# Last projection pair out of the stage's pool, heads split into even and odd, a later load of z, a longer wait in the gating's sums, and SiLU and splits of the projection as items of their own

## The chip, the cores and the metric

The kernel runs on one core of one Trainium2 chip. The metric is the device time of one execution in microseconds (us); several runs are taken and their median is given. A profile of one execution shows every engine: TensorE (PE, with its weight loads as PEld), VectorE (DVE), ScalarE (ACT), GpSimd (POOL), and SyncE (SP), whose queue issues the DMA transfers.

## What is computed

One inference step of one layer: a half-step SwiGLU feed-forward, a token mixer with two parallel branches, and a second half-step feed-forward, all with RMSNorm ahead and plain residual adds. There are 1024 prompt tokens of one sequence and 8 sequences with 8 sample tokens each, width 1024, feed-forward width 2816. All of it is in float32. The mixer is where the change lies:

```python
proj = hn @ w_in
u, z, xbc, dt_raw, gate_logits = ...            # 1024, 2048, 3072, 32, 2048 columns
branch_pool = pool_mix(u_ext, ...) @ pool_w_out # trailing-window means minus token, windows 2, 4, 8, 16
xbc_c, new_conv = causal_conv(xbc, ...)         # width 4, then SiLU
y, new_ssm = ssd_scan(xs, dt, A, bm, cm, ssm_h0)# 32 heads of 64 in 4 groups, chunks of 128 tokens
y = y + d_skip[:, None] * xs
yg = y * silu(z)
yg = yg * rsqrt(mean(yg * yg over a group) + EPS)
branch_ssd = (yg * ssd_norm) @ ssd_w_out
gates = sigmoid(gate_logits)
merged = gates[0] * branch_pool + gates[1] * branch_ssd
return merged @ w_o, new_pool, new_conv, new_ssm
```

The new states of the pooling, the convolution and the scan are outputs too.

## The kernel before

**Tiling.** Activations lie with features on the 128 partitions and tokens along the free axis, in two halves: h = 0 has 512 prompt tokens, h = 1 the other 512 and the 64 sample tokens, 576. A float32 product is made of three products of rounded high and low parts (`hi`, `lo` or `hl` of the activations, `wh` and `wl` of the weights). ACT makes `wh` (L443) and DVE `wl` (L444), each 128x512. The feed-forward's first matrix and the projection use one level of Winograd's form of Strassen's product: a pair of column blocks takes seven products in the order 1, 2, 6, 5, 7, 3, 4, and POOL makes the weights' sums `s` (L437) for four of them.

**Stages.** The first feed-forward runs to about 800 us, the projection to 1523 us, the mixing stage to 2125 us, and the second feed-forward to the end. The first two share one pool of buffers, in which `fx` takes one of 17 rotating tiles. The mixing stage opens a pool of its own in the same memory, so its first tiles wait for whatever was last read there. `act` takes tiles of the pool that lives through the whole program; in the mixing stage `fx` does so too.

**The projection** (`in_proj`, `proj_pair`). After `mix_dt` and some plain blocks come gate pairs, then for each of the 4 groups three convolution pairs ("c"), one pooling pair ("u") and two pairs of `z`, and at the end one gate pair for h = 1 alone. `proj_pair` asks for the seven products; `after` and `leave` evict each from PSUM as it ends (copies on ACT, additions on DVE, h = 0's sums on POOL) with a raised priority of 40 places in the program's order, as for `wh` and `wl`. When a block is whole, `done` puts an item on the list `work`: `post_conv` (for each block and half one ACT pass, three DVE passes L940 over the row `ct`, and SiLU on ACT L942 with a store), `post_u` (running sums `us` on DVE L955, on small tiles `urs` for the sample tokens L959, the difference `dd` L966, a split of it and two stores), `post_z`, `post_gate`, and `state_out` (PE transposes `pst` of the last rows, then stores).

**What sets the order.** `pe[0]` is a clock of PE's work as the program is written, counted by `mm`. Generators started as a `Chain` are stepped by `tick` when that clock passes their due time; the number that a generator yields is its wait. `worker` takes items of `work` in order, each not before RIPE us of that clock after it was posted. At the start of a pair `proj_pair` sets `hurry` and steps the worker until no more than 4 items are on the list; all that it records then stands ahead of the pair. A scheduler then lays out each engine's row from the recorded order and the priorities. Every engine, and SP's DMA queue, runs its row in order.

**The mixing stage.** `pool_branch` multiplies the differences `d` by the group weights (`pgm`), then by the output weights `pool_w_out` (`pbp`). Beside it runs the chain `scan`: for each half and group it fetches `dts`, `bc` (B and C rows) and `xs` (L1518 to L1526) and walks the chunks. `ssd_a` loads `ab`, the running sums of dt times A of the group's heads, broadcast to all partitions, from the scratch tensor `acs_d` (one tile of 4 heads at a time, two for a chunk) and makes of it `ea` (exponentials, one head per 64 partitions, L1355) and the decay matrices in `ab` itself (L1357, L1358); `ssd_b` makes `pyo` and `pyd` and the output; `ssd_st` makes the state `pst`. Gating multiplies by `z`, which `ssd_group` loads at the fourth chunk, and `rstd` sums squares over a group by the matmuls `pss` and waits for them. Then come `ssd_w_out` (`pso`), the merge of the branches (`acc`, L1595, and t1 = `t` L1608, L1609) and `w_o` (`pwo`).

Of the kernel before, what the change touches and what calls it, by code (L numbers as in the profile page):

```python
# [44 lines left out]
STEP_S = 1.0  # L45
POST, RIPE = 1.0, 3.0
GP = (1.5, 1.2)
# [14 lines left out]
def tile_hybrid_pool_ssd_macaron(  # L62
# [189 lines left out]
    acs_d = [dp.tile([4, NH, CH], F32, tag=f"acsd{h}", name=f"acsd{h}") for h in HALVES]  # L252
# [116 lines left out]
    def rstd(tiles, h, count, out, pace=1.0):  # L369

        N = NTOK[h]
        nch = 4 + h
        s = act((P, N), name="ssq")
        for i, x in enumerate(tiles):
            if i == 0:
                S.activation(s, x, AF.Square)
            else:
                q = act((P, N), name="sq")
                S.activation(q, x, AF.Square)
                V.tensor_tensor(s, s, q, op=ALU.add)  # L380
# [24 lines left out]
        yield R_WAIT  # L405
        out.append(r)
        yield 1.5
# [419 lines left out]
    def mix_dt(h, xs):  # L827
# [9 lines left out]
        def chain():  # L837
# [43 lines left out]
            dma(acs_d[h].rearrange("c h l -> (c h) l"), afm)  # L881
# [28 lines left out]
    def post(gen):  # L910
        work.append((pe[0] + RIPE, gen))
# [12 lines left out]
    def post_conv(h, ct, raw, new):  # L924
# [17 lines left out]
        S.activation(t[:, :N], t[:, :N], AF.Silu)  # L942
        dma(convd[h][ct], t[:, :N])
        yield POST / 2

    def post_u(h, k, raw, smp):
# [6 lines left out]
        while sh < w:  # L953
# [20 lines left out]
        yield POST  # L974
# [21 lines left out]
    def done(kind, i, h, raw):  # L996
# [13 lines left out]
        if kind == "c":  # L1010
            if h == 1:
                smp = new
                state_out(kind, i, raw[:, 512:579])
            post(post_conv(h, i, raw, smp))
        else:
            if h == 1:
                smp = hists.pop(("u", i))
                G.tensor_copy(smp[0][:, :, HIST:], new)
                state_out(kind, i, raw[:, 512:591])
            post(post_u(h, i, raw, smp))  # L1020
# [34 lines left out]
    def proj_pair(kind, ia, ib, xs):  # L1055
# [4 lines left out]
        while len(work) > 4:  # L1060
            poster[0].step()
# [16 lines left out]
        def after(p, i, bk):  # L1078
# [3 lines left out]
            if p == "1":  # L1082
                out[i] = {"a": fx(name="ra"), "b": fx(name="rb")}
# [216 lines left out]
    def ssd_a(h, g, c, Bf, Cf, xs4, dts, h0s):  # L1300
# [11 lines left out]
        for q in range(nq):  # L1312
            ab = act((P, hq, L), name="ab")
            if smp:
                dma(ab, acs_sd[g * HPG : (g + 1) * HPG].partition_broadcast(P))
# [35 lines left out]
        for q, ab in enumerate(abs_):  # L1351
            av = ab.rearrange("p (q h) l -> p q h l", h=2)
            ev = ea[:, q * (hq // 2) : (q + 1) * (hq // 2), :]
            for hh in range(2):
                S.activation(ev[hh * HD : (hh + 1) * HD], av[hh * HD : (hh + 1) * HD, :, hh, :], AF.Exp)  # L1355
            for i in range(hq):
                S.activation(ab[:L, i, :], ab[:L, i, :], AF.Relu, bias=acs[:L, hc + q * hq + i : hc + q * hq + i + 1], scale=-1.0)  # L1357
            S.activation(ab[:L], ab[:L], AF.Exp, scale=-1.0)  # L1358
            V.tensor_tensor(ab[:L], ab[:L], cbm[:L, :L].unsqueeze(1).broadcast_to([L, hq, L]), op=ALU.mult)  # L1359
# [10 lines left out]
    def ssd_b(h, g, c, a, hold, Cf, y4, dts, h0s):  # L1370
# [8 lines left out]
        if smp:  # L1379
# [12 lines left out]
            for i, (pr, bh) in enumerate(units):  # L1392
# [12 lines left out]
                dma(dst, h0)  # L1405
                if pr == 3:
# [19 lines left out]
        for i in range(HPG):  # L1426
            m_ = abs_[i // abs_[0].shape[1]][:L, i % abs_[0].shape[1], :]
# [31 lines left out]

    def ssd_group(h, g, Bf, Cf, xs4, dts, zs):  # L1460
# [3 lines left out]
        for c in range(4 + h):  # L1464
            ga = ssd_a(h, g, c, Bf, Cf, xs4, dts, h0s)
            next(ga)
            if c == 3:
                for j in range(4):
                    z = act((P, NTOK[h]), name="z")
                    dma(z, zd[h][g * 4 + j])  # L1470
                    zs.append(z)
# [5 lines left out]
            if prev:  # L1477
                yield from ssd_b(h, g, *prev, Cf, y4, dts, h0s)
            prev = (c, a)
        yield step  # L1480
        yield from ssd_b(h, g, *prev, ssd_st(h, g, *prev, dts), Cf, y4, dts, h0s)
# [9 lines left out]
    def gating(h, g, y4, zs, out):  # L1491
# [6 lines left out]
        yield from rstd([y4[:, j, :N] for j in range(4)], h, 512, rr, GP[0])  # L1498
# [56 lines left out]
    cs = start(scan())  # L1555

# [25 lines left out]
    def merge(h, gs, acc):  # L1582
# [18 lines left out]
        for m in range(KD):  # L1601
# [7 lines left out]
            V.tensor_tensor(t1[m], t1[m], acc[m], op=ALU.add)  # L1609
# [168 lines left out]
```

## Time and profile before

| what | before |
|---|---|
| median of 3 runs | 2938.1 us (2935.09 to 2938.73) |
| profiled execution | 2939.05 us |
| its span on the core | 2937.3 us |
| PE idle, 1000 to 1500 us (projection pairs) | 15.8 us |
| PE idle, 1523 to 2125 us (mixing stage) | 41.8 us |

A span is the time from the first to the last instruction of the profiled execution; the rest of its time lies around it. PE's idle time is the stretch less its busy time. A busy share is a mean over stages with different limits, so each stage is read by itself. In a list of waits a row has the waiting engine and line, what ended the wait, the sum of such waits in us, their number, and the longest. In a list of groups a row has line, engine, operation, tiles and shapes, count, then busy us and the mean of one in ns, then the idle time of the engine just before and what ended it. In a timeline a row has its start and duration in us, and in brackets the idle time of the engine before it.

### The profile page before, as it was taken

How to read it: one execution, taken by the hardware profiler on the slowest of the kernel's cores; microseconds unless marked ns; L12 is line 12 of the kernel's file. 1: busy time of each engine (PE TensorE's matmuls, PEld its weight loads, DVE VectorE, ACT ScalarE, POOL GpSimd, SP SyncE). 2: the span in 40 equal slices, each digit the busy share in tenths (PEclk: the TensorE clock that was granted, in tenths of full speed). 3: DMA queues.
4: the chain of work that ended last, by engine and by line, in shares of the span. 5: the costliest groups of instructions: out<-in, count | busy, mean ns of one | idle time of the engine just before them, and what ended most of it. 6: DMA issues, size and time to landing. Idle time of an engine off the chain costs nothing.

```text
span 2937.3 us, 51029 instructions
## 1 busy us (share of the span) xinstructions
PE 2828.8 (96%) x18494; PEld 2570.2 (88%) x18494; DVE 1784.7 (61%) x2843; ACT 1385.2 (47%) x3024; POOL 993.0 (34%) x1011
## 2 busy tenths in 40 slices
PE   7999999999999999999989999898999999999998
PEld 6999999789989989898977887677999999987898
DVE  6655555434484687887976877766665544453422
ACT  5444444323354555564556766566233444442422
POOL 6434444000133455454422332323234444440000
PEclk9999999999999999999999999999999999999999
DMA  4575554856445555543367777786774532236652
GB/s 134 166 224 182 160 172 132 277 188 194 112 126 163 159 179 159 183 127 124 98 221 240 235 235 232 229 271 184 237 241 153 161 98 77 81 101 212 218 156 72
DMA packets 530332, 507.97 MB, mean 173 GB/s; under 512 B 36884, under 2 KB 374664, under 8 KB 530072
## 3 DMA queue, kind: packets, MB, share of 16 engines
q1 hardware_dynamic: 530064, 504.72, 54.0%
q8 instruction: 145, 2.38, 0.3%
q14 instruction: 107, 0.88, 0.1%
q10 hardware_dynamic: 16, 0.00, 0.0%
HBM read 361.77 MB, written 143.05 MB: 172 GB/s over the span
## 4 chain that ended last, share of the span: by engine, by line
PE 44%; DVE 6%; ACT 3%; DMA 3%; issue 1%; POOL 1%; SPq 1%; POOLq 0%; ACTq 0%; DVEq 0%
PE pw L163 19%; PE po L163 9%; PE pso L163 4%; PE pwo L163 3%; PE pbp L163 3%; PE pg L163 1%; PE pu L163 1%; ACT ab L1357 1%; PE pyd L163 1%; DVE wl L444 1%; DVE ct L940 1%; PE pst L163 1%; DMA wraw<-in_ffn_w_in_dram 0%; DVE xs L1504 0%; DVE ab L1359 0%
## 5 line engine op out<-in xcount | busy, mean ns | idle before, releaser
L163 PE MATMUL pw<-X,wh 128*128 128x288 f32 (+1 forms) x2484 | 624.0, 330 | 11.9 <-ACT t L1120 5.3
L163 PE MATMUL pw<-X,wl 128*128 128x288 f32 (+1 forms) x1644 | 472.9, 288 | 0.8 <-DVE wl L444 0.8
L163 PEld LDWEIGHTS pw<-X,wh 128*128 128x128 f32 x2484 | 417.7, 188 | 51.5 <-ACT t L1120 6.7
L163 PE MATMUL pw<-hl,wh 128*128 128x512 f32 x1072 | 390.5, 398 | 3.1 <-DVE t L1129 2.1
L444 DVE TENSOR_TENSOR wl<-s,wh 128x512 fp32r<-128x512 f32 x288 | 223.3, 776 | 200.6 <-ACT wh L443 179.1
L163 PE MATMUL pw<-hi,wh 128*128 128x288 f32 x1120 | 332.1, 297 | 1.3 <-ACT t L596 1.3
L163 PE MATMUL pw<-lo,wh 128*128 128x288 f32 x1120 | 329.7, 294 | 0.0
L163 PE MATMUL pw<-hi,wl 128*128 128x288 f32 x1120 | 329.6, 294 | 0.0
L295 DVE TENSOR_TENSOR wl<-wraw,wh 128x512 fp32r<-128x512 f32 x228 | 164.2, 721 | 249.2 <-ACT wh L294 236.9
L163 PEld LDWEIGHTS pw<-X,wl 128*128 128x128 f32 x1644 | 310.6, 189 | 1.9 <-DVE wl L444 1.8
L437 POOL TENSOR_TENSOR s<-wraw,wraw 128x512 f32<-128x512 f32 x144 | 196.0, 1361 | 333.7 <-DVE wl L444 216.7
L163 PE MATMUL pw<-hl,wl 128*128 128x256 f32 x1072 | 299.6, 280 | 0.2 <-DVE wl L444 0.2
L294 ACT ACTIVATE wh<-wraw 128x512 fp32r<-128x512 f32 x228 | 137.8, 606 | 326.0 <-PE po L163 229.1
L444 DVE TENSOR_TENSOR wl<-wraw,wh 128x512 fp32r<-128x512 f32 x216 | 177.0, 819 | 123.0 <-ACT wh L443 116.3
L443 ACT ACTIVATE wh<-s 128x512 fp32r<-128x512 f32 x288 | 180.8, 629 | 146.4 <-PE pw L163 139.1
L163 PEld LDWEIGHTS pw<-hl,wh 128*128 128x128 f32 x1072 | 201.9, 188 | 40.6 <-DVE t L1129 2.9
L163 PEld LDWEIGHTS pw<-hi,wh 128*128 128x128 f32 x1120 | 210.1, 188 | 12.6 <-ACT t L596 1.8
L163 PE MATMUL po<-hh,wh 128*128 128x288 f32 (+1 forms) x800 | 211.0, 324 | 3.6 <-ACT hh L355 3.4
L163 PE MATMUL po<-hh,wl 128*128 128x288 f32 (+1 forms) x800 | 210.9, 322 | 0.5 <-DMA wl<-part 0.5
L163 PE MATMUL po<-hr,wh 128*128 128x288 f32 (+1 forms) x800 | 210.9, 323 | 0.0
L163 PEld LDWEIGHTS pw<-lo,wh 128*128 128x128 f32 x1120 | 210.2, 188 | 0.0
L163 PEld LDWEIGHTS pw<-hi,wl 128*128 128x128 f32 x1120 | 210.1, 188 | 0.0
(384 smaller groups left out, 6340.7 us busy)
## 6 DMA issues: line engine op xcount, KB each, us to landing
wraw<-in_ffn_w_in_dram SPq DMA_DIRECT2D x188, 256.0 KB
wh<-part SPq DMA_DIRECT2D x156, 256.0 KB
wl<-part SPq DMA_DIRECT2D x156, 256.0 KB
wraw<-in_w_in_dram SPq DMA_DIRECT2D x144, 256.0 KB
wraw<-in_ffn_w_out_dram SPq DMA_DIRECT2D x120, 256.0 KB
part<-ph SPq DMA_DIRECT2D x80, 256.0 KB
part<-pr SPq DMA_DIRECT2D x80, 256.0 KB
ab<-acsd SPq DMA_DIRECT2D x64, 256.0 KB
```

The source lines that it names most:

```text
L163: T.matmul(out, lhsT, rhs, start=start, stop=stop, skip_group_check=free)
L294: S.activation(wh, raw, AF.Copy)
L295: V.tensor_tensor(wl, raw, wh.bitcast(F32), op=ALU.subtract)
L437: G.tensor_tensor(t, a, b, op=op)
L443: S.activation(wh, a, AF.Copy)
L444: V.tensor_tensor(wl, a, wh.bitcast(F32), op=ALU.subtract)
L940: V.scalar_tensor_tensor(o, f(j), w[j], o, op0=ALU.mult, op1=ALU.add)
L1357: S.activation(ab[:L, i, :], ab[:L, i, :], AF.Relu, bias=acs[:L, hc + q * hq + i : hc + q * hq + i + 1], scale=-1.0)
```

## The change

1. The last gate pair, with one half only, takes its two blocks `ra` and `rb` from `act` in place of `fx`.
2. The convolution's SiLU and store, and the split of `dd` with its two stores, become items of their own, `conv_out` and `u_out`, put on the end of `work` with 1.5 in place of RIPE. RIPE goes from 3 to 4, and a pair's start leaves 5 items in place of 4. `state_out` is posted after `post_conv` or `post_u`. The small sums on `urs` move from DVE to POOL.
3. `acs_d` holds the even heads of a group ahead of the odd ones. It is written in 8 transfers per half in place of one; a tile `ab` has the even or the odd heads of a chunk (a sample chunk's one tile has both, loaded in 2 transfers), and `ea` takes one exponential of 64x512 for each in place of two of 64x256. `pyd` takes its heads from the two tiles in turn.
4. For h = 1 the four loads of `z` move from the fourth chunk into the sample chunk, after its unit 4's state store.
5. Gating's `rstd` waits 2.5 us more of the program's PE clock before it puts its sums on PE.
6. The chain `scan` is stepped once as soon as it is started, ahead of `pool_branch`.
7. In the merge, t1 + acc of h = 0 goes from DVE to POOL.

```diff
-POST, RIPE = 1.0, 3.0
-GP = (1.5, 1.2)
+STEP_S, Z_UNIT = 1.0, 4
+POST, RIPE, RIPE_2 = 1.0, 4.0, 1.5
+GP, G_WAIT = (1.5, 1.2), 2.5
...
-    acs_d = [dp.tile([4, NH, CH], F32, tag=f"acsd{h}", name=f"acsd{h}") for h in HALVES]
+    acs_d = [dp.tile([4, NG, 2, 4, CH], F32, tag=f"acsd{h}", name=f"acsd{h}") for h in HALVES]
...
-        yield 2.0 * max(pace, 0.75)
+        yield wait + 2.0 * max(pace, 0.75)
...
-            dma(acs_d[h].rearrange("c h l -> (c h) l"), afm)
+            for i in range(HPG):
+                dma(acs_d[h][:, :, i % 2, i // 2, :].rearrange("c g l -> (c g) l"), afm[i::HPG])
...
-    def post(gen):
-        work.append((pe[0] + RIPE, gen))
+    def post(gen, ripe=RIPE):
+        work.append((pe[0] + ripe, gen))
...
-        S.activation(t[:, :N], t[:, :N], AF.Silu)
-        dma(convd[h][ct], t[:, :N])
+        post(conv_out(h, ct, t[:, :N]), RIPE_2)
+
+    def conv_out(h, ct, t):
+        S.activation(t, t, AF.Silu)
+        dma(convd[h][ct], t)
         yield POST / 2
...
-                V.tensor_tensor(nxs[:, :, 2 * sh - 1 :], curs[:, :, 2 * sh - 1 :],
+                G.tensor_tensor(nxs[:, :, 2 * sh - 1 :], curs[:, :, 2 * sh - 1 :],
...
-        yield POST
+        post(u_out(h, k, dd, N), RIPE_2)
+
+    def u_out(h, k, dd, N):
         dh = fx(F32R, "dh")
         split(dd[:, :N], dh[:, :N], dd[:, :N].bitcast(F32R))
...
+            post(post_conv(h, i, raw, smp))
+            if h == 1:
                 state_out(kind, i, raw[:, 512:579])
-            post(post_conv(h, i, raw, smp))
...
-        while len(work) > 4:
+        while len(work) > 5:
             poster[0].step()
...
-                out[i] = {"a": fx(name="ra"), "b": fx(name="rb")}
+                new = act if len(xs) == 1 else fx
+                out[i] = {"a": new(name="ra"), "b": new(name="rb")}
...
-                r0 = g * HPG + q * hq
-                dma(ab, acs_d[h][c, r0 : r0 + hq].partition_broadcast(P))
+                dma(ab, acs_d[h][c, g, q].partition_broadcast(P))
...
-            for hh in range(2):
-                S.activation(ev[hh * HD : (hh + 1) * HD], av[hh * HD : (hh + 1) * HD, :, hh, :], AF.Exp)
-            for i in range(hq):
-                S.activation(ab[:L, i, :], ab[:L, i, :], AF.Relu, bias=acs[:L, hc + q * hq + i : hc + q * hq + i + 1], scale=-1.0)
...
+            S.activation(ea[hh * HD : (hh + 1) * HD], av[hh * HD : (hh + 1) * HD], AF.Exp)
+            for i in range(4):
+                k = hc + 2 * i + hh
+                S.activation(av[:L, i, :], av[:L, i, :], AF.Relu, bias=acs[:L, k : k + 1], scale=-1.0)
...
+                if i == Z_UNIT:
+                    load_z(h, g, zs)
...
-            m_ = abs_[i // abs_[0].shape[1]][:L, i % abs_[0].shape[1], :]
+            m_ = abs_[0][:L, i % 2 * 4 + i // 2, :] if smp else abs_[i % 2][:L, i // 2, :]
...
-            if c == 3:
-                for j in range(4):
-                    z = act((P, NTOK[h]), name="z")
-                    dma(z, zd[h][g * 4 + j])
-                    zs.append(z)
+            if c == 3 and h == 0:
+                load_z(h, g, zs)
...
-        yield from rstd([y4[:, j, :N] for j in range(4)], h, 512, rr, GP[0])
+        yield from rstd([y4[:, j, :N] for j in range(4)], h, 512, rr, GP[0], G_WAIT)
...
     cs = start(scan())
+    cs.step()
...
-            V.tensor_tensor(t1[m], t1[m], acc[m], op=ALU.add)
+            (V if h else G).tensor_tensor(t1[m], t1[m], acc[m], op=ALU.add)
```

How the rows of the engines change is shown at three places. A name's number is that of its buffer and differs between the two programs.

**SP's queue at the change to the mixing stage.** `zd` and `gd` are the last stores of the projection, `wraw` weights, `ab` the scan's loads, `dts`, `bc` and `xs` the fetch of a chunk's rows. Before:

```order
L921 DMA zd_15_183<-rb_17334 128x512
L291 DMA wraw_17886<-in_pool_w_group_dram 128x2x256
L921 DMA zd_15_199<-rb_17355 128x576
L291 DMA wraw_17917<-in_pool_w_out_dram 128x4x128
L291 DMA wraw_17939<-in_pool_w_out_dram 128x4x128
L291 DMA wraw_17962<-in_pool_w_out_dram 128x4x128
L291 DMA wraw_18018<-in_pool_w_out_dram 128x4x128
L916 DMA gd_4_220<-ra_17602 128x576
L291 DMA wraw_18055<-in_pool_w_out_dram 128x4x128
L916 DMA gd_5_221<-rb_17603 128x576
L1318 DMA ab_17773<-acsd_115 128x512
L1318 DMA ab_17775<-acsd_115 128x512
```

and after:

```order
L922 DMA zd_14_182<-ra_17366 128x512
L922 DMA zd_14_198<-ra_17384 128x576
L291 DMA wraw_17933<-in_pool_w_out_dram 128x4x128
L922 DMA zd_15_183<-rb_17367 128x512
L922 DMA zd_15_199<-rb_17385 128x576
L1539 DMA dts_17750<-dtp_272 128x576
L1531 DMA bc_17752<-cv_16_136 128x512
L1532 DMA bc_17753<-cv_20_140 128x512
L1534 DMA xs_3228_17754<-cv_0_120 128x512
L1534 DMA xs_3228_17754<-cv_1_121 128x512
L1534 DMA xs_3228_17754<-cv_2_122 128x512
L917 DMA gd_4_220<-ra_17616 128x576
```

The fetch from `dts` on stood behind six loads of output weights, both gate stores and the two `ab`; now it stands behind one such load and ahead of the gate stores. Five loads of output weights, which stood before it, now follow the second fetch and the `ab`, ahead of the `d` loads of the third pooling group.

**DVE at the start of the third convolution pair of the first group.** `wl` are the low parts of the pair's weights, `ct` the convolution's rows (`crs` are the sample tokens), `t` and `ra` the pair's evictions, `rb` the last eviction of the pair ahead. Before:

```order
L1136 TENSOR_TENSOR rb_11240<-pw_2070_11230,t_11241 128x256
L940 SCALAR_TENSOR_TENSOR ct_11466<-crs_11467,cols,ct_11466 128x64
L444 TENSOR_TENSOR wl_11574<-wraw_11525,wh_11573 128x512
L940 SCALAR_TENSOR_TENSOR ct_11512<-ra_11239,cols,ct_11512 128x512 x2
L444 TENSOR_TENSOR wl_11618<-s_2145_11615,wh_11617 128x512
L940 SCALAR_TENSOR_TENSOR ct_11512<-ra_11239,cols,ct_11512 128x512
L940 SCALAR_TENSOR_TENSOR ct_11549<-ra_11263,cols,ct_11549 128x512
L940 SCALAR_TENSOR_TENSOR ct_11549<-crs_11550,cols,ct_11549 128x64
L940 SCALAR_TENSOR_TENSOR ct_11549<-ra_11263,cols,ct_11549 128x512
L940 SCALAR_TENSOR_TENSOR ct_11549<-crs_11550,cols,ct_11549 128x64
L1122 TENSOR_TENSOR t_11546<-pw_2137_11577,t_11546 128x512
L444 TENSOR_TENSOR wl_11648<-s_2144_11613,wh_11647 128x512
```

and after:

```order
L444 TENSOR_TENSOR wl_11565<-wraw_11556,wh_11564 128x512
L941 SCALAR_TENSOR_TENSOR ct_11522<-ra_11244,cols,ct_11522 128x512
L941 SCALAR_TENSOR_TENSOR ct_11527<-ra_11263,cols,ct_11527 128x512
L941 SCALAR_TENSOR_TENSOR ct_11522<-ra_11244,cols,ct_11522 128x512
L941 SCALAR_TENSOR_TENSOR ct_11527<-crs_11528,cols,ct_11527 128x64
L941 SCALAR_TENSOR_TENSOR ct_11522<-ra_11244,cols,ct_11522 128x512
L941 SCALAR_TENSOR_TENSOR ct_11527<-ra_11263,cols,ct_11527 128x512
L941 SCALAR_TENSOR_TENSOR ct_11527<-crs_11528,cols,ct_11527 128x64
L941 SCALAR_TENSOR_TENSOR ct_11527<-ra_11263,cols,ct_11527 128x512
L941 SCALAR_TENSOR_TENSOR ct_11527<-crs_11528,cols,ct_11527 128x64
L444 TENSOR_TENSOR wl_11603<-wraw_11558,wh_11602 128x512
```

Before, two to six rows stand between one `wl` and the next; now nine do, the whole of two convolutions, and the third `wl` follows eight rows later.

**PE at the sums of a gating of the first half** (at 1767 us of the profile before). `pso` is the out-projection, `pss` the sums of squares, `pyo` and `pyd` the scan's next chunk. Before:

```order
L163 MATMUL pso_20505<-yhl_19401,wh_20506 128x512 x2
L163 MATMUL pso_20505<-yhl_19401,wl_20508 128x512
L163 MATMUL pso_20505<-yhl_19430,wh_20506 128x512
L163 MATMUL pss_20496<-ones,ssq_20398 128x1 x4
L163 MATMUL pso_20505<-yhl_19430,wh_20506 128x512
L163 MATMUL pso_20505<-yhl_19430,wl_20508 128x512
L163 MATMUL pyo_20516<-bc_19684,hst_20361 128x128 x4
L163 MATMUL pyd_20521<-ab_20323,xdt_20376 64x128 x4
```

and after:

```order
L163 MATMUL pyo_20487<-bc_19674,hst_20341 128x128 x4
L163 MATMUL pyd_20492<-ab_20303,xdt_20356 64x128
L163 MATMUL pyd_20492<-ab_20305,xdt_20356 64x128
L163 MATMUL pyd_20492<-ab_20303,xdt_20356 64x128
L163 MATMUL pyd_20492<-ab_20305,xdt_20356 64x128
L163 MATMUL pyd_20492<-ab_20303,xdt_20356 64x128
L163 MATMUL pyd_20492<-ab_20305,xdt_20356 64x128
L163 MATMUL pyd_20492<-ab_20303,xdt_20356 64x128
L163 MATMUL pyd_20492<-ab_20305,xdt_20356 64x128
L163 MATMUL pss_20508<-ones,ssq_20376 128x1 x4
L163 MATMUL pso_20473<-yhl_19557,wh_20474 128x512 x2
L163 MATMUL pso_20473<-yhl_19557,wl_20476 128x512
```

The sums stood ahead of the chunk's `pyo` and `pyd` and now stand behind them.

More of the change, by code (lines that the diff above doesn't have):

```diff
@@ L44 @@
 STEP = (5.0, 3.8)
-STEP_S = 1.0
-POST, RIPE = 1.0, 3.0
-GP = (1.5, 1.2)
+STEP_S, Z_UNIT = 1.0, 4
+POST, RIPE, RIPE_2 = 1.0, 4.0, 1.5
+GP, G_WAIT = (1.5, 1.2), 2.5
 HN_AT, HN_PACE = 25.0, 2.0
@@ L367, in along, with rstd @@
         tr(out, r[:n, i : i + 1].broadcast_to([n, P]), ident[:n, :n])
-    def rstd(tiles, h, count, out, pace=1.0):
+    def rstd(tiles, h, count, out, pace=1.0, wait=0.0):
         N = NTOK[h]
@@ L1368, in load_state, with ssd_b @@
         return t
-    def ssd_b(h, g, c, a, hold, Cf, y4, dts, h0s):
+    def ssd_b(h, g, c, a, hold, Cf, y4, dts, h0s, zs):
         dt, acs, dtd, cd, cdp = dts
@@ L1458, in ssd_st, with load_z @@
         return hold
+    def load_z(h, g, zs):
+        for j in range(4):
+            z = act((P, NTOK[h]), name="z")
+            dma(z, zd[h][g * 4 + j])
+            zs.append(z)
     def ssd_group(h, g, Bf, Cf, xs4, dts, zs):
@@ L1477, in ssd_group @@
             if prev:
-                yield from ssd_b(h, g, *prev, Cf, y4, dts, h0s)
+                yield from ssd_b(h, g, *prev, Cf, y4, dts, h0s, zs)
             prev = (c, a)
         yield step
-        yield from ssd_b(h, g, *prev, ssd_st(h, g, *prev, dts), Cf, y4, dts, h0s)
+        yield from ssd_b(h, g, *prev, ssd_st(h, g, *prev, dts), Cf, y4, dts, h0s, zs)
         if h == 1:
```

15 lines of the change are left out of this document (8 added, 7 removed).

## The prediction

> **What bounds the kernel now.** I read the busy times first, then the busy time by stage, then who waits for whom on PE, then two places of the timeline.
>
> ```profile
> PE 2828.8 (96%) x18494; PEld 2570.2 (88%) x18494; DVE 1784.7 (61%) x2843; ACT 1385.2 (47%) x3024; POOL 993.0 (34%) x1011
> ```
>
> ```profile
> 1000.00:1500.00 500.00, 484.18 (x3190) 448.71 (x3189) 425.73 (x664) 274.29 (x562) 248.65 (x299) 1.00 0.45 144
> 1500.00:1600.00 100.00, 90.33 (x504) 75.02 (x503) 58.68 (x89) 55.32 (x125) 21.47 (x17) 0.93 0.78 252
> 1523.00:2125.00 602.00, 560.24 (x3800) 470.16 (x3801) 417.03 (x648) 354.98 (x910) 177.35 (x138) 0.97 0.73 235
> ```
>
> The first fence is PE's and the other engines' busy time in the whole span; in the second the columns after the stretch are its length, then the busy time of PE, PEld, DVE, ACT and POOL, then the granted clock. PE is the bound everywhere, so an edit is worth only the PE idle time that it takes away or makes, and the clock lost with it. There are two pools of such time where the edits lie. In the projection pairs (1000 to 1500 us) PE idles 500 − 484.2 = 15.8 us, while DVE is busy 425.7 of 500 us, 85%: next to PE it is the engine with least room. In the mixing stage (1523 to 2125) PE idles 602 − 560.2 = 41.8 us, and its clock is 0.97. The feed-forward stages are not touched. What PE waits for, in total, times and longest:
>
> ```profile
> PE pst L167 <- DVE ra L1114: 6.7, 8, 1.4
> ...
> PE pss L163 <- DVE ssq L380: 5.9, 3, 2.7
> PE pw L163 <- ACT t L1120: 5.3, 5, 3.0
> ...
> PE pyd L163 <- ACT btok L1336: 2.8, 2, 1.7
> ...
> PE pw L163 <- DVE wl L444: 1.0, 3, 0.5
> ```
>
> The last row matters most below: in the whole program PE loses only 1.0 us to a late low part of a Winograd weight (`wl`). DVE makes these parts, and before the change they come in time.
>
> **The start of the mixing stage.** SP issues every load in its order, and there the order is bad:
>
> ```profile
> 1513.92 8.26 SPq L291 DMA_DIRECT2D wraw<-in_pool_w_out_dram  x4
> ...
> 1523.92 0.51 SPq L916 DMA_DIRECT2D gd<-rb  x1
> ...
> 1529.31 0.32 SPq L1526 DMA_DIRECT2D dts<-dtp  x1
> ...
> 1536.77 0.32 SPq L1188 DMA_DIRECT2D d<-dh  x1
> ```
>
> ```profile
> 1523.85 0.62 PE L163 MATMUL pgm<-d,wh 128*128 128x512 f32 x2
> 1524.30 0.40 PE L163 MATMUL pgm<-d,wl 128*128 128x512 f32 x1
> ...
> 1535.16 0.44 PE L167 MATMUL pxT<-ident,xs 128*128 128x128 f32 x1 [3.65 <-DMA xs<-cv]
> ...
> 1542.59 1.39 PE L163 MATMUL pgm<-d,wh 128*128 128x512 f32 x2 [4.34 <-DMA d<-dh]
> ...
> 1547.99 0.40 PE L163 MATMUL pbp<-fh,wh 128*128 128x512 f32 x1
> ```
>
> Four loads of output weights occupy SP for 8.26 us, the last gate store follows, and the chunk's tiles (`dts`, then `bc` and `xs`) come only from 1529.31 on, since the pool memory they take belonged to the last pair. PE then idles 3.65 and 4.34 us, the brackets in the rows. After the second gap twelve `pgm` matmuls take 1547.99 − 1542.59 = 5.40 us, while ahead of the gap two took 1524.30 − 1523.85 = 0.45, so twelve would take 2.7: another 2.7 us lost to a lower clock. Together 3.65 + 4.34 + 2.7 = 10.7 us. After the change the fetch of the chunk stands ahead of all but one of the output weights and of the gate stores, the last pair's blocks lie elsewhere, and the 24 `pgm` ready at the start (5.4 us at 0.225) cover what is left of the loads. Bounds: 0 (the `d` loads still queue) to −10.7; I take **−10**, as both late loads move ahead by more than the gaps they caused.
>
> **The other edits in the mixing stage.** Three of the gaps there, with what follows:
>
> ```profile
> 1767.45 1.02 PE L163 MATMUL pss<-ones,ssq 128*128 128x1 f32 x8 [2.21 <-DVE ssq L380]
> ...
> 1768.88 1.07 PE L163 MATMUL pyo<-bc,hst 128*128 128x128 f32 x8
> 1769.89 1.97 PE L163 MATMUL pyd<-ab,xdt 128*64 128x128 f32 x16
> ```
>
> ```profile
> 1875.19 0.50 PE L163 MATMUL pwo<-mh,wh 128*128 128x512 f32 x1 [3.11 <-DVE t L1608]
> ...
> 1875.88 0.63 PE L163 MATMUL pwo<-mh,wl 128*128 128x512 f32 x1
> ...
> 1878.87 0.47 PE L163 MATMUL pwo<-mh,wh 128*128 128x512 f32 x1
> ```
>
> The longer wait of the gating puts the `pss` sums behind the next chunk's `pyo` and `pyd` (1.07 + 1.97 = 3.0 us of PE, more than the 2.21 gap). Bounds −5.9 (the row of waits) to 0. The same scan work stood behind `pss` before and lies ahead of it now, so the sums must only be ready 3 us later: **−5.5**.
>
> `pwo` waits 3.11 us for a merge on DVE, and then seven matmuls take 1878.87 − 1875.88 = 2.99 us where seven at 0.225 take 1.6: 1.4 us more of clock. The change gives eight additions of this merge to POOL:
>
> ```profile
> L1609 DVE TENSOR_TENSOR t<-t,acc 128x512 f32<-128x512 f32 x8 | 8.5, 1068 | 1.6 <-POOL acc L1595 1.4
> ...
> L1595 POOL TENSOR_TENSOR acc<-acc,ac 128x512 f32<-128x512 f32 x8 | 11.3, 1411 | 20.2 <-DVE acc L1594 16.1 <-DMA ab<-acsd 4.2
> ```
>
> On POOL one costs 1.41 us in place of 1.07 (that row is the same addition of the same shape), +0.34 in the chain, but it no longer queues behind DVE's scan work. Between −4.5 and +8 × 0.34 = +2.7: **−3.5**.
>
> ```profile
> L1355 ACT ACTIVATE ea<-ab 64x256 f32<-64x256 f32 x136 | 55.9, 411 | 15.0 <-DMA ab<-acsd 13.4
> ...
> L1358 ACT ACTIVATE ab<-ab 128x512 f32<-128x512 f32 x64 | 39.5, 618 | 0.1
> ```
>
> Even and odd heads apart let 128 exponentials of 64x256 be 64 of 64x512. The nearest row for the wide form is 0.618 us, so 64 × 0.618 + 8 × 0.411 = 42.8 us in place of 55.9: 13 us off ACT. ACT is busy 355 of 602 us here, so most of it lies beside PE; what PE waits for on this chain is the `pyd` row, 2.8 us. I take **−2**. Against it, each `pyd` now needs both `ab` tiles from its second matmul on, and the `z` loads of the second half stand behind the state stores on SP:
>
> ```profile
> SPq L1405 <- DVE h L1403: 27.7, 24, 6.8
> ```
>
> SP stood still up to 6.8 us there, and the gating's product waits for `z`, `pss` and the out-projection behind it. From 0 to +6.8: **+2**, since 24 waits of 27.7 us are 1.2 us each. The mixing stage sums to −10 − 5.5 − 3.5 − 2 + 2 = **−19**.
>
> **The projection pairs.** Here the change moves work within DVE's row, and this is where it can lose.
>
> ```profile
> L444 DVE TENSOR_TENSOR wl<-s,wh 128x512 fp32r<-128x512 f32 x86 | 70.3, 820 | 17.6 <-ACT wh L443 16.2 <-PE pw L163 1.3
> L940 DVE SCALAR_TENSOR_TENSOR ct<-rb,cols,ct 128x512 f32<-128x512 f32 x72 | 62.7, 871 | 11.5 <-ACT ct L936 11.1
> L444 DVE TENSOR_TENSOR wl<-wraw,wh 128x512 fp32r<-128x512 f32 x66 | 59.7, 905 | 16.5 <-ACT wh L443 15.0 <-DMA wraw<-in_w_in_dram 1.2
> ...
> L940 DVE SCALAR_TENSOR_TENSOR ct<-crs,cols,ct 128x64 f32<-128x64 f32 x70 | 31.2, 445 | 0.0
> ...
> L1129 DVE TENSOR_TENSOR t<-pw,t 128x512 f32<-128x512 f32 x22 | 15.0, 681 | 0.5 <-PE pw L163 0.5
> ...
> L1114 DVE TENSOR_TENSOR ra<-pw,ra 128x288 f32<-128x288 f32 x22 | 9.8, 447 | 3.2 <-PE pw L163 3.2
> ...
> L955 DVE TENSOR_TENSOR us<-us 128x524 f32<-128x524 f32 x11 | 9.0, 822 | 0.0
> ```
>
> ```profile
> ACT ct L942 <- DVE ct L940: 63.4, 40, 3.9
> ACT dh L355 <- DVE dd L970: 16.8, 6, 4.5
> ```
>
> *Gain.* ACT's SiLU and the split of `dd` stand in ACT's row up to 3.9 and 4.5 us ahead of their data, and the evictions (`t`) queue behind them: 5.3 us of PE. As items of their own, 1.5 us later, they are ready when ACT comes to them. The small sums on `urs` leave DVE, and the transposes `pst` are posted later, which answers the 6.7 us. Of the 15.8 us idle here I take **−13**: both rows (12.0) and one of the rest; at worst 0.
>
> *Loss.* Finishing a convolution now appends an item, so the list at a pair's start does not get shorter until whole convolutions have been run: they are recorded in one lump ahead of the pair's weights. The order of DVE at the third pair of each group shows it: between the first `wl` and the second stand six full and three small `ct` rows; with the `wl` itself 6 × 0.84 + 3 × 0.445 + 0.905 = 7.3 us. PE has 24 matmuls between the first uses of the two; at 484.18 us for 3190, 0.152 us each, that is 3.6. Late by 3.6. To the third `wl` it is four full `ct`, a small one, an eviction of 0.68, one of 0.45 and the `wl`: 3.4 + 0.45 + 0.68 + 0.45 + 0.82 = 5.8 us against 17 matmuls, 2.6. Late by 3.2, so 6.8 a group, 27 in four. The lower bound is 0, if DVE comes to the lump that much earlier. How far ahead it runs shows in its waits:
>
> ```profile
> DVE wl L444 <- ACT wh L443: 83.2, 59, 2.8
> ```
>
> It waits 83.2 / 59 = 1.4 us for a `wh` where it waits at all. With that lead at each of the two, 6.8 − 2.8 = 4.0 a group: **+16**. At the first `z` pairs the same happens with the `us` and `dd` rows of the pooling branch. In the last group eleven large and three small of them and five `wl` stand between a `wl` and the fifth after it: 11 × 0.82 + 3 × 0.445 + 5 × 0.82 = 14.5 us, against 57 matmuls, 8.7: 5.8 late. The other three lumps are shorter, by their rows some 3 us late at most: 14 in full, 0 at the least. In a `z` pair DVE has few other rows and comes early, so I take **+5**. The pairs sum to −13 + 16 + 5 = **+8**.
>
> By a rule of the Trainium skill (TensorE: Matmul & The Clock Gate, Part 1: The HAM clock gate) PE falls to half its clock after an idle window of about 3.4 us and needs about as long a busy one to come back. The half rate in the rows above agrees, 5.40 us for 2.7 us of work; but here it also came after 3.11 us of idling, so the trace is stricter than the rule. By the rule a stall of 2 us at a lump would cost no clock; by the rows it may, 1.4 us each, and only the rival below has that in its sum.
>
> **The sum.** The profiled execution took 2939.05 us, span 2937.3; the median of the runs is 2938.1, so 1 us lower. 2939.05 − 19 + 8 = 2928, against the median **2927**. The 1.8 us around the span stay.
>
> **Rivals.**
>
> *The lumps bite in full* (slower). DVE has no lead at a lump, because the row ahead of it is the last eviction of the pair before, for which it waits on PE. Then the pairs give −13 + 27 + 14, and four of the stalls over 3 us cost 1.4 us of clock each, 5.6: +33.6 − 19 = +14.6, **2953**. It decides from where lumps and clock together pass 32 us. For it: DVE is busy at 85%, and the `wl` rows now stand right ahead of their use. Against it: the lump takes away rows that would have filled the next 20 us of DVE, and PE does the products with `wh` first.
>
> *The lumps are hidden* (faster still). DVE is far enough ahead, 0 in place of 16 + 5: −32, **2906**. For it the 1.0 us of today's waits for `wl`; against it the same row, which is for an order with `wl` well ahead.
>
> *The mixing stage keeps its waits.* Five loads of output weights now stand ahead of the `d` loads, and if they hold SP as the four did (8.26 us), the 4.34 us and its 2.7 of clock remain: −3 in place of −10; and if `pss`, moved back, delays the out-projection of its group, −5.5 becomes −1. Then −19 + 7 + 4.5 + 8 = +0.5, **2939**. For it, what SP did before; against it, that PE comes to these `d` after more other work than before.
>
> **How the numbers follow.** Forecast 0.36 (2918 to 2936), lumps in full 0.25, hidden 0.26, waits kept 0.13. A measurement of this kernel tells 0.2%, 5.9 us, from no change. Faster: 0.26 and nine tenths of the forecast, 0.33, and of the third rival nothing: 0.59. Same: the rest of the forecast, 0.03, and 0.11 of the third rival, 0.14. Slower: 0.25 and 0.02, 0.27. The signs are mixed, so the range reaches into both outer rivals, 2904 to 2956; the forecast's own is 2918 to 2936.
>
> **What would show it.** In the changed profile: no gap over 2 us at the start of the mixing stage, `dts` issued by about 1516, PE busy over 96 us in the stretch 1500 to 1600 at a clock near 1.00; `pss` gone from PE's waits; `pwo`'s first gap under 1 us. In the pairs: the rows `pst` and `pw <- ACT t` gone, and a new row `pw <- DVE wl` of some 15 to 20 us in 20 or so waits, at the third pair of each group. If that row is under 5 us the second rival is right; at 30 or more, and PE idle in the pairs above 35 us, the first. I am wrong beyond all of these if idle time appears in a stage that the change leaves alone, or if the late `z` holds the gating for more than 6.8 us a group.

## The result, and the profile after

The changed kernel took 2971.4 us, median of 4 runs (2967.5 to 2972.3), where the kernel before took 2937.6 (4 runs). The ratio is 1.0114, with an interval of 1.0096 to 1.0131: 34 us slower, where 11 us faster was forecast and the range ended at 2956. The profiled execution is one of 2967.5 us, span 2965.7.

The busy time by stage, with the columns as before (length, PE, PEld, DVE, ACT, POOL, granted clock, DMA share and rate):

```profile
1000.00:1500.00 500.00, 469.08 (x3041) 432.95 (x3040) 379.54 (x611) 266.48 (x539) 253.97 (x312) 0.98 0.42 136
1500.00:1554.00 54.00, 46.71 (x304) 43.87 (x303) 33.19 (x55) 24.96 (x49) 12.21 (x12) 0.94 0.58 191
1554.00:2156.00 602.00, 562.23 (x3824) 472.87 (x3825) 425.62 (x648) 344.38 (x854) 190.38 (x147) 0.97 0.74 235
```

In the projection pairs PE now idles 500 − 469.1 = 30.9 us where it was 15.8, and its clock is 0.98 where it was 1.00. The mixing stage of the same length idles 39.8 us, before 41.8. Over the whole of the pairs, with nearly the same number of matmuls in both stretches (3181 and 3182), the changed kernel takes 530 us where the kernel before takes 498; after and before:

```profile
1016.00:1546.00 530.00, 492.11 (x3181) 454.36 (x3181) 395.95 (x639) 275.11 (x558) 257.28 (x315) 0.98 0.44 143
```

```profile
1016.00:1514.00 498.00, 482.18 (x3182) 447.14 (x3181) 422.37 (x660) 271.85 (x559) 245.07 (x295) 1.00 0.46 149
```

PE idles 530 − 492.1 = 37.9 us there, before 498 − 482.2 = 15.8, so some 22 of the 32 us are idle time. The other 492.1 − 482.2 = 9.9 are slower matmuls: the granted clock stood at half for 23.9 us in all, before for 3.4. PE's waits in the whole span show what came and what went:

```profile
PE pw L163 <- DVE wl L444: 14.3, 14, 1.8
...
PE pgm L163 <- DVE fl L359: 7.6, 3, 4.1
PE pw L163 <- ACT v L1134: 7.0, 1, 7.0
PE pw L163 <- ACT t L1136: 5.8, 1, 5.8
PE pw L163 <- ACT t L1129: 5.7, 4, 2.9
...
PE pss L163 <- DVE ssq L380: 4.4, 2, 3.2
...
PE pwo L163 <- DVE t L1622: 1.8, 1, 1.8
PE pgm L163 <- DMA d<-dh: 1.7, 1, 1.7
```

The row of `wl` went from 1.0 to 14.3 us; two single stalls of 7.0 and 5.8 us on ACT's evictions are new; `pgm <- DVE fl` went from 2.9 to 7.6. The 6.7 us of `pst <- DVE ra` are gone, with 2.0 of `pst <- ACT so` in their place, and so is `pxT <- DMA xs` at 4.4. The row `pw <- ACT t` of the kernel before, 5.3 us at L1120, has stayed: it is the one of 5.7 at L1129.

Both kernels run 18494 matmuls, so the start of the n-th one can be set against the start of the n-th one before. That puts the loss in its places (us; the differences between rows are what was lost or won in between). The two profiled executions part by 28 us, the medians by 34, since that of the changed kernel was the shortest of its four runs.

```
n       before    after    after - before
6300    1013.0   1012.5     -0.5
6500    1045.0   1048.3     +3.4   third convolution pair, group 0
7200    1153.4   1156.5     +3.1
7300    1168.3   1177.4     +9.1   third convolution pair, group 1
7500    1201.3   1207.4     +6.1
7600    1217.3   1228.3    +11.0   first z pair, group 1
8000    1279.6   1288.3     +8.7
8200    1309.3   1322.2    +12.8   third convolution pair, group 2
8400    1341.3   1353.6    +12.3
8500    1357.4   1377.7    +20.3   first z pair, group 2
8900    1417.9   1437.4    +19.5
9000    1433.4   1458.0    +24.6   third convolution pair, group 3
9200    1465.2   1487.8    +22.6
9300    1484.8   1516.4    +31.6   first z pair, group 3
9500    1514.1   1545.7    +31.6   end of the projection
10000   1617.2   1639.2    +22.0   start of the mixing stage
10100   1633.1   1661.5    +28.4
13500   2143.7   2171.4    +27.8
```

The first `z` pair of group 0 lies between n = 6600 (+2.9) and 6700 (+4.4). The projection pairs lost 32 us; the mixing stage first won 9.5 and gave 6.4 of them back at once.

**A third convolution pair.** DVE and then PE, in the second group (a timeline: start, duration, and in brackets the idle time before):

```profile
1163.98 0.67 DVE L444 TENSOR_TENSOR wl<-wraw,wh 128x512 fp32r<-128x512 f32 x1
1164.59 2.06 DVE L941 SCALAR_TENSOR_TENSOR ct<-rb,cols,ct 128x512 f32<-128x512 f32 x3
1166.57 0.67 DVE L1131 TENSOR_TENSOR t<-pw,t 128x512 f32<-128x512 f32 x1
1167.17 0.73 DVE L941 SCALAR_TENSOR_TENSOR ct<-rb,cols,ct 128x512 f32<-128x512 f32 x1
1167.83 0.44 DVE L1115 TENSOR_TENSOR ra<-pw,ra 128x288 f32<-128x288 f32 x1
1168.20 0.38 DVE L941 SCALAR_TENSOR_TENSOR ct<-crs,cols,ct 128x64 f32<-128x64 f32 x1
1168.50 0.68 DVE L444 TENSOR_TENSOR wl<-s,wh 128x512 fp32r<-128x512 f32 x1
```

```profile
1164.71 0.39 PE L163 MATMUL pw<-hl,wl 128*128 128x256 f32 x1 [0.76 <-DVE wl L444]
...
1166.13 0.30 PE L163 MATMUL pw<-hi,wh 128*128 128x288 f32 x1
1166.26 0.29 PE L163 MATMUL pw<-lo,wh 128*128 128x288 f32 x1
...
1169.23 0.38 PE L163 MATMUL pw<-X,wl 128*128 128x256 f32 x1 [1.75 <-DVE wl L444]
...
1170.91 0.68 PE L163 MATMUL pw<-X,wh 128*128 128x288 f32 x2
1171.39 0.44 PE L163 MATMUL pw<-X,wl 128*128 128x288 f32 x1
```

Between two `wl`, here the second and the third of the pair, stands the lump of convolution rows that the order shows, without a gap, and PE starts as soon as the second `wl` is there, 1.75 us late, after 0.76 us at the first. From 1170.91 on a 288-column step takes 0.24 us (1171.39 − 1170.91 = 0.48 for two), where one took 1166.26 − 1166.13 = 0.13: the granted clock is 0.50 from 1170.3 to 1173.7.

**A first z pair.** PE's longest new stall, in the last group, and the engines that it waits for:

```profile
1510.18 0.80 PE L163 MATMUL pw<-X,wh 128*128 128x512 f32 x1 [6.97 <-ACT v L1134]
```

```profile
1509.06 0.59 ACT L1136 COPY t<-pw 128x512 f32<-128x512 f32 x1 [7.75 <-POOL ra L1132]
1509.54 0.59 ACT L1134 COPY v<-pw 128x512 f32<-128x512 f32 x1
```

```profile
1507.82 1.20 POOL L1132 TENSOR_TENSOR ra<-t 128x256 f32<-128x256 f32 x1 [3.39 <-DVE dd L974]
```

```profile
1502.62 3.10 DVE L959 TENSOR_TENSOR us<-us 128x524 f32<-128x524 f32 x3
1505.75 0.69 DVE L970 SCALAR_TENSOR_TENSOR dd<-us,rb 128x512 f32<-128x512 f32 x1
1506.36 0.70 DVE L959 TENSOR_TENSOR us<-rb 128x526 f32<-128x526 f32 x1
1506.98 0.17 DVE L973 TENSOR_TENSOR dd<-us,invcnt 128x15 f32<-128x15 f32 x1
1507.06 0.68 DVE L1131 TENSOR_TENSOR t<-pw,t 128x512 f32<-128x512 f32 x1
```

Read backwards: PE has no PSUM until ACT has copied out two products; ACT's copy into `t` waits 7.75 us until POOL has read the old `t`; POOL waits for DVE's addition into it (L1131); and that stands behind the pooling's lump on DVE. Here `wl` is not late at all. An eviction is. The stall of 5.8 us in the third group has the same chain; in the first two groups the first `z` pairs have only shorter stalls, for `wl` 1.6 and 1.3 us and for an eviction 2.5.

### The profile page after: what moved, and what is told of

Read it like the earlier page. It is cut to its first block, busy times and chain, and to the rows that moved or that the text cites. A ratio compares the mean times of both kernels' runs of the same rounds, so it can differ in the third digit from the quotient of the medians.

```text
span 2965.7 us, 51047 instructions
## 1 busy us (share of the span) xinstructions
PE 2838.9 (96%) x18494; PEld 2577.3 (87%) x18494; DVE 1764.2 (59%) x2819; ACT 1377.3 (46%) x2964; POOL 1018.3 (34%) x1039
## 4 chain that ended last, share of the span: by engine, by line
PE 80%; DVE 8%; DMA 4%; ACT 4%; issue 2%; POOL 1%; SPq 1%; POOLq 0%; ACTq 0%; DVEq 0%
PE pw L163 43%; PE po L163 17%; PE pso L163 5%; PE pg L163 3%; PE pwo L163 3%; PE pbp L163 2%; PE pu L163 2%; PE pyd L163 1%; DVE ct L941 1%; DMA hr<-hd 1%; DVE us L959 1%; ACT ab L1365 1%; DVE wl L444 1%; DVE xs L1517 1%; DVE wl L295 1%
## 5 line engine op out<-in xcount | busy, mean ns | idle before, releaser
L163 PE MATMUL pw<-X,wh 128*128 128x288 f32 (+1 forms) x2484 | 631.3, 333 | 21.1 <-ACT v L1134 7.0
```

The lines of the kernel that those rows point to most:

```text
L163: T.matmul(out, lhsT, rhs, start=start, stop=stop, skip_group_check=free)
```

## The experiments

All runs were set against runs of the kernel before on the same chip; ratios are to those.

### The items in line again

```diff
-        post(conv_out(h, ct, t[:, :N]), RIPE_2)
+        yield from conv_out(h, ct, t[:, :N])
...
-        post(u_out(h, k, dd, N), RIPE_2)
+        yield POST
+        yield from u_out(h, k, dd, N)
```

> SiLU with its store and the split of dd stand again inside post_conv and post_u; all other edits stay. Theory A (the lump: a drained convolution or pooling item appends another, so the drain at a pair's start records whole blocks ahead of the pair): the 32 us that the projection lost go, the first pgm of the mixing stage starts at 1510 to 1523 us in place of 1554.6, and the time is 2920 to 2938. Rival B (the later posting, RIPE 4 and five items left, makes blocks and evictions late whatever the items are): the time stays at 2960 to 2972.

Measured: 2940.2 us, ratio 1.0006 (0.9996 to 1.0015). The first `pgm` starts at 1522.56:

```profile
1522.56 0.73 PE L163 MATMUL pgm<-d,wh 128*128 128x512 f32 x2 [0.92 <-ACT rb L1126]
```

The 32 us of the projection are gone, though RIPE is 4 and five items may stay. B falls. The time is 2 us above what A gave; the mixing stage's edits are worth nothing together, as the fourth run shows. PE still waits 12.7 us for `wl` in these pairs, hardly less than the changed kernel's 14.3. What went is the waits for ACT's evictions, 21.0 us in four rows there and 4.0 here, and the half clock, 23.9 us there and 3.4 here.

### The drain counts blocks only

```diff
-        work.append((pe[0] + ripe, gen))
+        work.append((pe[0] + ripe, gen, ripe == RIPE))
...
-        while len(work) > 5:
+        while sum(q[2] for q in work) > 5:
```

> The items stay apart, but the drain at a pair's start counts only the blocks' own items, not the SiLU and split items. Theory A: the same as with the items in line, 2920 to 2938, and the row pw <- DVE wl under 3 us. Rival C (the items apart are themselves the loss, since they put SiLU and split in ACT's row where evictions wait): 2955 to 2972. Rival B: 2960 to 2972.

Measured: 2934.2 us, ratio 0.9987 (0.9978 to 0.9996). The items apart do no harm as such: C falls. The projection is now shorter than before, `pgm` starting at 1514.75 where it was 1523.04. But PE still waits for `wl`, 7.1 us in small pieces, where A expected under 3:

```profile
PE pw L163 <- DVE wl L444: 7.1, 13, 1.5
PE pw L163 <- ACT t L1129: 1.5, 3, 1.1
```

### RIPE 3

```diff
-POST, RIPE, RIPE_2 = 1.0, 4.0, 1.5
+POST, RIPE, RIPE_2 = 1.0, 3.0, 1.5
```

> RIPE is 3 again as before; all other edits stay. Theory A: the drain runs whatever RIPE says, so 2962 to 2975. Rival B (blocks started too late): most of the loss goes, 2930 to 2945.

Measured: 2971.0 us, ratio 1.0117 (1.0100 to 1.0134). RIPE has no part in the loss.

### The mixing edits alone

All edits of the projection's items undone, as the expectation lists them.

> All edits of the projection's items are undone (items in line, RIPE 3, four items left, order of state_out, small sums on DVE); the last pair's blocks, the heads, z, the gating's wait, the early fetch and the merge stay. If the mixing edits are worth what the matched matmuls of the two profiles show, 3.8 us: 2930 to 2936. If they are worth the forecast 19 us and the projection's loss disturbed them: 2915 to 2922.

Measured: 2939.9 us, ratio 1.0005 (0.9996 to 1.0015). Both expectations were too good: the mixing stage's edits together, the gating's wait among them, are worth nothing. By the n-th matmul, worked out as above, the start of the stage wins 6.9 us from n = 9500 to 10000, and 5.3 are lost to n = 10100, at this stall:

```profile
PE pgm L163 <- DVE fl L359: 7.6, 3, 4.1
```

So the loss inside the mixing stage does not come from the late projection.

### The items apart, alone, on the kernel before

The two posts of the first experiment, with RIPE 3 and four items left; nothing else of the change.

> The kernel before with one edit alone: SiLU and store, and the split of dd, as items of their own, 1.5 after the rest; RIPE 3 and four items left. Theory A (an item that appends an item makes the drain record whole blocks in a lump): slower than before by 15 us or more, 2952 to 2985, with pw <- DVE wl over 8 us. Rival (the lump needs the change's other numbers too): 2930 to 2945.

Measured: 2945.2 us, ratio 1.0021 (1.0010 to 1.0031). Slower, with 19.0 us of `wl` waits, but by 6 us and not by 15 or more. The items apart alone don't make 32 us.

### Only one kind of item apart

The first experiment's convolution line alone, then its pooling lines alone.

> The changed kernel with the convolution's SiLU in line again; the pooling's split stays apart. If the lumps at the first z pairs (some 23 us by the matched matmuls) are made by the pooling's own items: 2955 to 2966. If they are made by the convolution's items, which stand on the list ahead of them: 2930 to 2942.

> The changed kernel with the pooling's split in line again; the convolution's SiLU stays apart. If each kind of item makes its own lumps: some 19 us lost at the third pairs and the z pairs repaired, 2945 to 2955. If the convolution's items make both: 2962 to 2972.

Measured: with only the pooling's items apart 2948.3 us (1.0027, 1.0016 to 1.0038); with only the convolution's 2968.4 us (1.0097, 1.0082 to 1.0112). The convolution's items make both kinds of lump: at the first z pairs the list still holds them, ahead of the pooling's blocks. The first of the two came out 6 us above what that needed, and the reason is not known.

### Four items left

```diff
-        while len(work) > 5:
+        while len(work) > 4:
```

> The changed kernel with the drain down to four items again, in place of five. In its order one of 214 wl stands six matmuls or less ahead of its first use, in the changed kernel's 18, in the kernel before none. Theory A2 (what a drain records depends on what stands at the list's head when it reaches its limit; with five left it must run through a whole row of blocks before the appended items let the list get shorter): most of the 32 us go, 2936 to 2948. Rival (a deeper drain records more, so more is lost): 2972 or more.

Measured: 2945.4 us, ratio 1.0027 (1.0016 to 1.0039). One number gives back 26 of the 34 us. How that can be shows when the drain's steps are counted while the program is written out. In each group, steps that the drain records at the start of the second and third convolution pair, the pooling pair and the first z pair (its lowest and highest over the groups), and the start of the first `pgm` in the profile:

```
                                 c2   c3    u   z1       first pgm, us
before                            5    8    8    6 to  9    1523.0
changed                           0   20    0   11 to 20    1554.6
items in line                     0    8    8    8          1522.6
drain counts blocks               0    6    8    8          1514.8
items apart alone                 5   16    5    7 to 16    1530.4
only pooling apart                0    8    8    8          1529.8
only convolution apart            0   20    0   12 to 18    1553.4
four left                         9    9    9    3 to  9    1528.1
state_out first                   0   20    0   11 to 20    1549.9
```

When the second pair starts, exactly five items are on the list (three convolutions, two `state_out`), so a limit of five drains nothing. At the third pair there are ten. From there each convolution that is finished appends its SiLU, the list gets no shorter by it, and only after 20 steps, four convolutions, does it fall to five. The next pair finds five again. With a limit of four the work is spread, nine steps at each of three pairs and 3 to 9 at the first `z` pair.

Every run with 20 steps at a pair's start has its `pgm` at 1549 us or later (RIPE 3 and the small sums on DVE too, with the changed kernel's steps); every run with 16 or fewer at 1530.4 or earlier. The clock in the pairs goes the same way: it stood at half for 20.5 to 27.3 us in the runs with 20 steps, for 13.7 in the one with 16, and for 0 to 6.8 in the others. Below 20 steps the count doesn't order the runs: items in line and only pooling apart have the same steps at these four pairs, and lie 7 us apart.

### state_out first, and the small sums on DVE

```diff
-            post(post_conv(h, i, raw, smp))
             if h == 1:
                 state_out(kind, i, raw[:, 512:579])
+            post(post_conv(h, i, raw, smp))
```

> The changed kernel with state_out posted ahead of post_conv and post_u, as before. In its order five of 214 wl stand that near to their use, one at the start of each group's third pair. Theory A2 (the head of the list decides): a part of the loss goes, 2945 to 2962. Rival (state_out has no part in it): 2967 to 2973.

> The changed kernel with the 20 small sums on DVE again. In its order 24 of 214 wl stand that near to their use. Theory A2: same loss or a little more, 2965 to 2982. Rival E (on POOL the small sums stand ahead of the additions that let ACT reuse t, and make the 7 us stalls at the first z pairs): 2950 to 2962.

Measured: 2967.7 us (1.0110, 1.0091 to 1.0129) and 2966.2 us (1.0101, 1.0086 to 1.0116). Neither edit makes the loss; each is worth a few us at most. The first was a miss of A2: only five `wl` stand close to their use there, and yet the loss stays, because its drains are the same 20 steps. The evictions are late, and `wl` costs no less than in the changed kernel (15.6 us, there 14.3):

```profile
PE pw L163 <- ACT v L1132: 15.6, 3, 7.2
PE pw L163 <- DVE wl L444: 15.6, 11, 3.0
```

How near `wl` stands to its use was the wrong measure; the size of the largest drain tells the runs with the whole loss from the others. Rival E falls with the second.

### Without the gating's wait, and without the early fetch

On the kernel whose drain counts blocks:

```diff
-GP, G_WAIT = (1.5, 1.2), 2.5
+GP, G_WAIT = (1.5, 1.2), 0.0
```

> The drain counts only the blocks' own items, and the gating's wait is 0 as before. Theory D (the longer wait moves the first gating's yhl rows on ACT and DVE between the pgm evictions of the second half, which makes the new stall pgm <- DVE fl of 4.06 us and its clock): that stall goes, the pss waits of 5.9 us come back; 2929 to 2935. Rival (the early fetch of the scan moves them there): the 4 us stall stays and pss comes back, 2937 to 2943.

Measured: 2925.1 us, ratio 0.9949 (0.9934 to 0.9963). This is the best run, 14 us faster than before, 9 us faster than with the wait (2934.2), and 4 us under what the expectation gave. PE's waits in the mixing stage, without the wait and then with it:

```profile
PE pst L163 <- DVE xd L1356: 6.5, 3, 4.0
PE pss L163 <- DVE ssq L380: 4.6, 3, 1.9
PE pyd L163 <- ACT btok L1345: 3.5, 1, 3.5
PE pyd L163 <- DVE ab L1367: 2.9, 2, 1.9
PE pgm L163 <- DVE fl L359: 2.8, 2, 1.6
```

```profile
PE pgm L163 <- DVE fl L359: 5.2, 2, 4.0
PE pst L163 <- DVE xd L1356: 5.1, 3, 3.1
...
PE pss L163 <- DVE ssq L380: 4.3, 2, 3.1
```

The wait won 0.3 us of `pss`, and made the 4.0 us of `pgm`. ACT's row of the changed kernel shows how:

```profile
1647.89 0.71 ACT L355 ACTIVATE yhl<-xs,cols 128x512 fp32r<-128x512 f32 x1
1650.83 0.72 ACT L355 ACTIVATE yhl<-xs,cols 128x512 fp32r<-128x512 f32 x1 [2.22 <-DVE xs L1517]
1651.45 1.66 ACT L355 ACTIVATE fh<-pgm,cols 128x288 fp32r<-128x288 f32 x4
```

What follows the sums in the gating, `yhl`, came later too and now stands in ACT's row ahead of the evictions `fh` of `pgm`; it waits for DVE, and PE waits for its PSUM. D holds in the stall that goes: by the n-th matmul the run with the wait loses 5.5 us between n = 10000 and 10100, the run without it none. The rest of the 9 us has no place that the two profiles show, for these two executions lie only 4 us apart; and `pss` came back with 4.6 us, not 5.9.

```diff
     cs = start(scan())
-    cs.step()
```

> The drain that counts blocks, no longer wait in the gating, and the scan's first fetch not ahead of pool_branch (the best run so far without the early fetch, 2925.1 with it). If the early fetch is worth the 6 to 10 us that the matched matmuls show at the stage's start: 2931 to 2936, with gaps of 3 to 4 us at pxT and pgm back. If the last pair's blocks outside the stage's pool did it: 2924 to 2927.

Measured: 2927.7 us, ratio 0.9969 (0.9956 to 0.9981), against 2925.1 with the early fetch. Between the two expectations: the fetch is worth some 2.5 us, less than the two medians' spread makes sure; by the n-th matmul the start of the stage (n = 9500 to 10000) wins 3.0 us without it and 6.1 with it. A `pgm` gap of 2.57 us is back, the one at `pxT` is not, which fits the last pair's blocks outside the stage's pool doing their part without it; that edit was not taken out by itself. The heads, the later `z` and the merge on POOL were not run singly, nor was the gating's wait taken out of the changed kernel itself.

## Why the prediction was wrong, by its steps

- **The reading of the bound, and the place of the risk, held.** PE bounds, and the loss is in the pairs, at the eight places that the order showed. The size did not: 11 us faster was forecast, and 34 us slower came out.
- **The third pairs (+16)** came near by number, in part by luck. By the n-th matmul the four lost 3.9, 6.0, 4.1 and 5.1, 19 us. The lead of DVE that I subtracted is there: the stalls for `wl` are 0.5 to 0.8 and 1.8 us, 2.3 to 2.6 a group where I took 4.0. The rest is in good part the clock, which I had put into the rival alone: in three of the four groups it fell to half for 3.4 us, 1.7 us lost each time.
- **The first z pairs (+5)** are the step that failed. They lost 1.5, 4.9, 8.0 and 8.9, 23 us, more than the 14 that I had for their lumps in full. I took them low because "in a `z` pair DVE has few other rows and comes early". That looks at `wl`; what stalls PE in the last two groups, for 5.8 and 7.0 us, is the addition of product 2 on DVE, then POOL, then ACT's copy, a chain of three engines that one late DVE row holds up. At each of the two the clock was at half for 6.8 us. Of the evictions I had spoken at the third pairs alone, as two rows on DVE; behind them I saw no chain.
- **The old stalls of the pairs (−13)** came near by number: 32.1 lost in all, 42.5 at the eight places, so 10.4 won elsewhere. Only one of its two rows went, though. `pst <- DVE ra`, 6.7 us, is down to 2.0 of `pst <- ACT so`; the 5.3 us of `pw <- ACT t`, which the items apart were to answer, are 5.7 after the change, all of them in first `z` pairs. They are 0.6 with the items apart alone, 1.5 where the drain counts blocks and 2.0 with the items in line, so it isn't the items apart by themselves that decide over them.
- **The pairs** come to +32 where I had +8. That is near the first rival's +33.6, but not by its sum: it had 41 us of late `wl`, and the row of `wl` is 14.3; evictions and clock made up the rest.
- **The start of the mixing stage (−10)** was right: from n = 9500 to 10000 the difference falls by 9.5, and by 6.9 with the mixing stage's edits alone.
- **The gating's wait (−5.5)** had the wrong sign. I let only the sums move. All that follows them in the gating moved as well, and met the evictions of `pgm`: +9 by the runs with and without it, on the kernel whose drain counts blocks. The sums themselves still cost 4.4 us of 5.9. The third rival named "moved back" as the danger, but for the out-projection, and for 4.5 us.
- **The merge (−3.5)** was too much: the first `pwo` gap went from 3.11 to 1.79 us, and a second one from 0.88 to 1.41:

```profile
1900.83 0.79 PE L163 MATMUL pwo<-mh,wh 128*128 128x512 f32 x1 [1.79 <-DVE t L1622]
```

- **Heads and z (−2, +2)** weren't told apart by runs. By the profiles neither moved its row much: `pyd <- ACT btok` is 2.9 us after 2.8, and SP's waits for `h` at the state stores are 29.4 us after 27.7. The mixing stage in all: from +31.6 to +27.8, −3.8 where I had −19.
- The lumps' price hung on a number I had not looked at: I took the drain's lumps for a result of the items apart. They are that together with a limit of five that meets a list of five.

## What to carry to other kernels

A loop that drains a list "until it is short enough" should not count what the drained work itself appends. Here that cost most together with a limit equal to the length that the list has by itself: one drain does nothing and the next does twice the work. Either alone cost less: the limit with the items in line nothing, the items apart with the old limit 6 us. When a row of work is moved ahead of a pair on a busy engine, follow the evictions too, over all engines that share their buffer: one late row there held PE for 7 us, a late weight part for 1.8. A wait that covers one stall moves everything behind it in its chain; look where that lands.

## What was not expected of the hardware

The clock fell after short waits: at 1170 us two of them, 0.76 and 1.75 us, 4.5 us apart, came before steps of 0.24 in place of 0.13 us. The Trainium skill (TensorE: Matmul & The Clock Gate, Part 1: The HAM clock gate) has about 3.4 us of idling for it; the trace is stricter, and decides. So stalls far below 3 us can cost clock as well when they come close together, and the granted clock of 0.98 in the pairs is a loss beside the idle time. They don't always: in the third group two waits of 0.54 and 1.76 us, as far apart, brought no fall, and what tells the two cases apart isn't shown. And the same `ct` row took 0.69 us in the lumps (2.06 us for three) where its mean was 0.81 to 0.87 in the kernel before. The mean hides two kinds of rows: of the 142 `ct` rows of 128x512 between 1000 and 1520 us of the profile before, 116 took 0.65 to 0.72 us, and 22 took over 1.0, each of them beside a row of POOL. Short rows ran beside POOL too, so that this is the cause isn't shown. It is one more reason for `wl` being less late than I had worked out from the mean.
